# A depthwise convolution cut into steps and emitted between the weight products of its mixer

## The chip, the cores and the metric

The kernel runs on one core of a Trainium2 chip. The metric is the time of one execution on the device, in microseconds (us). The engines are written as the profile writes them: PE (matrix products; PEld its weight loads), DVE (vector engine), ACT (scalar engine), POOL (GpSimd), SP (here only the issuer of weight transfers). The engines run side by side; each works through its own instructions strictly in order and waits where it needs another engine's result.

## What is computed

The program is two two-layer transformer blocks over 256 rows of width 1024, in float32. The change touches one piece, the mixer of the second layer of the second block (the "odd mixer"):

```
def odd_mixer(u, conf_dw, conf_dw_b, conf_ln_g, conf_ln_b, sc_dw):
    a, gate, sb, scc, sx = jnp.split(u, [512, 1024, 1536, 2048], axis=-1)
    conf = a * jax.nn.sigmoid(gate)
    conf = depthwise_conv(conf, conf_dw) + conf_dw_b            # 31 taps
    conf = jax.nn.silu(group_layer_norm(conf, conf_ln_g, conf_ln_b, 4))
    sc = sb * depthwise_conv(scc * sx, sc_dw)                   # 3 taps
    return jnp.concatenate([conf, sc], axis=-1)
...
mix = odd_mixer(h @ b_w_in[j], ...) @ b_w_out[j]                # 1024x2560, 1024x1024
x = x + g1 * mix
```

## The kernel before

`phase_f` holds this layer. A float32 product is made of three products of rounded parts. So each weight tile of 1 MB (`w`, a ring of 4 slots, filled from SP's queue) is cut in two sub-steps, and each sub-step is **split**: ACT writes the rounded half `whi` (line 200), then POOL or DVE writes the rest `wlo` = `w` - `whi` (line 201, 128x1024). Three buffers of each are held (`NSPL`), so at most three sub-steps are split ahead of PE. In `lin_T` POOL does the `wlo` of every sub-step; in `residual` (through `products`) DVE does it. After each weight tile one step of a background job is pumped in: eight products `ada<-w,cs` with a 1 MB tile of their own; after eight steps comes `ada_sb` (DVE), then four transposes of it on PE, then `adaT` (DVE).

The input product `h @ b_w_in` goes as five calls of `lin_T`, each of two weight tiles, four sub-steps, 96 products of 256 columns: **c2=0** (gate and value of channel groups 0 and 1), **c2=1** (groups 2 and 3), **scc**, **sx**, **sb**. I number their sub-steps s1 to s4 (of c2=1), scc1 to scc4, sx1 to sx4, sb1 to sb4. A channel group is 128 channels on the partitions with the 256 rows beside each other, so a tap of the convolution is one DVE instruction over 128x256 (`SCALAR_TENSOR_TENSOR ocv<-oconf,cw,ocv`, line 1916): shifted input times the tap's weight plus the sum so far. Two of the 31 taps (`TAPS`) go over PE instead (`oconv<-odw,oconf`, line 1939), one is a DVE `TENSOR_SCALAR` with the bias (line 1918), 28 are left per group. They are emitted in the evictions: when the value of two groups is ready, DVE makes `oconf` = value * sigmoid(gate) (line 1934) and then all the taps of these two groups. The three-tap convolution `osv` is emitted in the eviction of sx in the same way.

After all five calls the sums `ocv` of the four groups are added onto PE's part in PSUM (line 1963, transposing them), `head_norm` normalizes 128 rows x 4 groups at a time (statistics, a reciprocal root of 10 small instructions on `hr_t`, `hr_y`, `hr_a`, then `oct`), PE transposes back (`oT`), ACT applies Silu (`osl`), and the result is split into `lhs_hi` and `lhs_lo` for `residual`. That one multiplies by `b_w_out`, four weight tiles in the order (half of the columns, first row block) = (0,4), (1,4), (0,0), (1,0); rows 4 to 7 come from `osv`, 0 to 3 from the normalized groups. I call its eight sub-steps r1 to r8 (12 products of 512 columns each).

A scheduler orders the emitted instructions engine by engine, so the order on an engine is near the order of emission but not the same.

Of the kernel before, what the change touches and what calls it, by code (L numbers as in the profile page):

```python
# [132 lines left out]
class Kernel:  # L133
# [23 lines left out]
    def rsqrt(self, v, eps, shape, scale=1.0, name="rs", bufs=4):  # L157

        nc = self.nc
        t = self.small(shape, name + "_t", bufs=bufs)  # L160
        y = self.small(shape, name + "_y", bufs=bufs)
        a = self.small(shape, name + "_a", bufs=bufs)
# [57 lines left out]
    def products(self, W, nk, steps, lhs, tts, evict):  # L220
# [4 lines left out]
        for c, cols, k0, kn in steps:  # L225
# [6 lines left out]
            for s0 in range(k0, k0 + kn, sub):  # L232
# [5 lines left out]
                for tt in tts:  # L238
# [1384 lines left out]
    def residual(self, W, nk, lhs, L, which):  # L1623

        nc = self.nc
        self.pump_to(self.ada[2 + L], 1 + which)
        with self.pool("res") as p:
            o = 2048 + 3072 * which
            g = self.bcast(p, self.ada[2 + L].dram[0, o:o + 1024], D, "gres")

            def ev(c, tt, ps):
                sl = slice(c * 512, c * 512 + 512)
                gy = self.sb.tile([128, 512], F32, name="gy", tag="s512")
                nc.vector.tensor_mul(gy, ps, g[:, sl])
                (nc.vector if c in RA else nc.gpsimd).tensor_add(self.xres[tt][:, sl], self.xres[tt][:, sl], gy)
            if nk == 8:
# [216 lines left out]
    def lin_T(self, W, cols, lhs, evict, eng):  # L1853
# [6 lines left out]
        for k0 in range(0, 8, per):  # L1860
            w = self.wtile(W, k0, per, cols)
            self.pump(self.rate)
            for s0 in range(0, per, sub):
                wh, wl = self.split(w[:, s0:s0 + sub], sub, n, eng)
                for k in range(sub):
                    kk = k0 + s0 + k
                    for c in range(n // 128):
# [2 lines left out]
                        nc.tensor.matmul(o, wh[:, k, cs], hi[:, kk], start=kk == 0 and c % 2 == 0, stop=False)  # L1870
                        nc.tensor.matmul(o, wh[:, k, cs], lo[:, kk], start=False, stop=False)  # L1871
                        nc.tensor.matmul(o, wl[:, k, cs], hi[:, kk], start=False, stop=kk == 7 and c % 2 == 1)  # L1872
        for i, a in enumerate(acc):
            evict(i, a)

    def phase_f(self):
# [3 lines left out]
        with ExitStack() as s:  # L1880
# [5 lines left out]
            with self.pool("pf") as p:  # L1886
# [13 lines left out]
                pv = [self.psB("oconv") for _ in range(2)]  # L1900
# [8 lines left out]
                scc = p.tile([128, 4, 256], F32, name="oscc")  # L1909

                def conv(dst, src, c, taps, w0, bias):
                    for k in taps:
                        w = cw[:, c, w0 + k:w0 + k + 1]
                        x = src[:, c, k:k + 256]
                        if k > taps[0]:
                            V.scalar_tensor_tensor(dst[:, c], x, w, dst[:, c], op0=OP.mult, op1=OP.add)  # L1916
                        elif bias is not None:
                            V.tensor_scalar(dst[:, c], x, w, bias, op0=OP.mult, op1=OP.add)
                        else:
                            V.tensor_scalar(dst[:, c], x, w, None, op0=OP.mult)  # L1920

                def each(ev):
                    def pair(i, ps):
# [4 lines left out]
                def ev_conf(c2):  # L1928
                    def ev(i, ps):
# [2 lines left out]
                            nc.scalar.activation(sg[:, c], ps, AF.Sigmoid)  # L1932
                            return
                        V.tensor_mul(conf[:, c, 15:271], ps, sg[:, c])
                        conv(cv, conf, c, range(TAPS, 31), 0, self.pcol[:, 53 + c:54 + c])
                        for t in range(2):
                            for k in range(TAPS):
                                at = k + t * 128
                                nc.tensor.matmul(pv[t][:, c * 128:c * 128 + 128], conf[:, c, at:at + 128],
                                                 dw[:, c, k], start=c == 0 and k == 0, stop=False)  # L1940
# [4 lines left out]

                def ev_sx(c, ps):
                    V.tensor_mul(scx[:, c, 1:257], ps, scc[:, c])
                    conv(sv, scx, c, range(3), 31, None)

                def ev_sb(c, ps):  # L1950
                    V.tensor_mul(sv[:, c], ps, sv[:, c])
                    self.split_T(mix[0][:, 4 + c], mix[1][:, 4 + c], sv[:, c])

                for c2 in range(2):
                    self.lin_T(W, ((512 + 256 * c2, 256), (256 * c2, 256)), lhs, each(ev_conf(c2)), nc.gpsimd)
                self.lin_T(W, ((1536, 512),), lhs, each(ev_scc), nc.gpsimd)
# [3 lines left out]
                ct = [p.tile([128, 512], F32, name=f"oct{t}") for t in range(2)]  # L1960
                for t in range(2):
                    for c in range(4):
                        nc.tensor.matmul(pv[t][:, c * 128:c * 128 + 128], cv[:, c, t * 128:t * 128 + 128],
                                         self.ident, start=False, stop=c == 3)
                    self.head_norm(pv[t], ct[t], True, 1e-6)
                for c in range(4):
                    po = self.psB("oT")
                    for t in range(2):
                        self.tr(po[:, t * 128:t * 128 + 128], ct[t][:, c * 128:c * 128 + 128])
                    u = self.sb.tile([128, 512], F32, name="osl", tag="s512")  # L1970
                    nc.scalar.activation(u[:, :256], po[:, :256], AF.Silu, scale=self.pcol[:, 57 + c:58 + c],
                                         bias=self.pcol[:, 61 + c:62 + c])
                    self.split_T(mix[0][:, c], mix[1][:, c], u[:, :256])
            self.residual(I["b_w_out_2"][0], 8, mix, 1, 0)
            for t in range(2):
                self.dump("x2_mid1", self.xres[t], t)
            self.ffn(1)
# [1 line left out]
    def build(self, s, upto="all"):  # L1979
# [62 lines left out]
```

## Time and profile before

| | |
|---|---|
| median of 3 runs | 2436.0 us (2433.91 to 2442.73) |
| the profiled execution: its time, and the span from first to last instruction | 2441.86 us, 2439.7 us |
| busy share of PE, DVE, ACT, POOL | 91%, 51%, 29%, 22% |
| mean granted clock of PE | 0.951 of full speed |

The shares are means over the whole program. What the changed stage is worth has to be read from its own stretch, from about 2111 us (the first two groups of the convolution can begin) to about 2241 us (the next layer part begins). All times below are us from the start of the span.

### The profile page before, as it was taken

Reading aid. Unit: us, or ns where it says so; the run is one execution under the profiler, and the core shown is the slowest. Engines: PE = TensorE matmul, PEld = TensorE weight load, DVE = VectorE, ACT = ScalarE, POOL = GpSimd, SP = SyncE. Lnnn points to the kernel's source line nnn. Section 1 sums busy time; section 2 is a strip of 40 time slices with the busy share of each in tenths; the row PEclk is TensorE's granted clock in tenths of the full one; section 3 lists DMA queues with packets and bytes.
Section 4 is the critical chain, followed back from the end, with each engine's and each line's share of the span. In section 5 each row is a group of like instructions: output and inputs, shape, how many; then the busy total and the mean of one; then the engine's idle time right before and its main releaser. Section 6 shows DMA issues by size and latency. Waiting matters only on the chain. (4 is left out here: it accounts for less than half of the span.)

```text
span 2439.7 us, 35230 instructions
## 1 busy us (share of the span) xinstructions
PE 2218.6 (91%) x13185; PEld 1395.5 (57%) x13186; DVE 1254.7 (51%) x2724; ACT 708.4 (29%) x1179; POOL 537.6 (22%) x451
## 2 busy tenths in 40 slices
PE   7999995789999998899779999998899999858999
PEld 3786673444444443676633333332655998657997
DVE  3354767444444444757842322223774554666554
ACT  2215242111111111434421111111453543414442
POOL 2121334233333333300130211111201000561000
PEclk9999996699999999899979999999899999979999
DMA  8654365389999999443569999999554555737553
GB/s 301 249 193 156 134 213 223 129 342 408 408 409 409 409 408 373 155 173 132 191 240 384 409 408 408 409 409 380 190 191 172 191 176 186 261 107 274 186 179 120
DMA packets 209272, 652.36 MB, mean 267 GB/s; under 512 B 20668, under 2 KB 33965, under 8 KB 197568
## 3 DMA queue, kind: packets, MB, share of 16 engines
q1 hardware_dynamic: 201680, 632.24, 68.9%
q0 software_dynamic: 7408, 17.73, 2.2%
q8 instruction: 107, 1.75, 0.3%
q14 instruction: 77, 0.63, 0.1%
HBM read 648.65 MB, written 1.25 MB: 266 GB/s over the span
## 5 line engine op out<-in xcount | busy, mean ns | idle before, releaser
L825 PE MATMUL gu<-w,xT 128*32 128x512 f32 (+1 forms) x2880 | 493.0, 605 | 16.2 <-PEq L967 9.9
L201 DVE TENSOR_TENSOR wlo<-w,whi 128x1024 fp32r<-128x1024 f32 (+3 forms) x240 | 298.7, 1246 | 308.6 <-ACT whi L200 308.4
L200 ACT ACTIVATE whi<-w 128x1024 fp32r<-128x1024 f32 (+3 forms) x264 | 274.2, 1041 | 508.4 <-PE A L247 276.8
L825 PEld LDWEIGHTS gu<-w,xT 128*32 128x32 f32 (+1 forms) x2880 | 141.0, 121 | 315.5 <-issue 246.4
L1872 PE MATMUL A<-lhs_hi,wlo 128*128 128x256 f32 x864 | 246.5, 286 | 14.1 <-POOL wlo L201 13.6
L246 PE MATMUL A<-wlo,lhs_hi 128*128 128x512 f32 (+3 forms) x640 | 248.7, 389 | 9.5 <-DVE wlo L201 9.4
L245 PE MATMUL A<-whi,lhs_hi 128*128 128x512 f32 (+3 forms) x640 | 250.6, 396 | 5.9 <-ACT whi L200 2.8
L1870 PE MATMUL A<-lhs_hi,whi 128*128 128x256 f32 x864 | 247.8, 287 | 1.0 <-ACT whi L200 1.0
L1871 PE MATMUL A<-lhs_lo,whi 128*128 128x256 f32 x864 | 247.1, 286 | 0.0
L247 PE MATMUL A<-whi,lhs_lo 128*128 128x512 f32 (+3 forms) x640 | 246.6, 386 | 0.0
L876 POOL TENSOR_TENSOR mx<-mx,gy 128x512 f32<-128x512 f32 x124 | 161.5, 1331 | 355.0 <-DVE gy L875 354.9
L851 PE MATMUL ey<-w,hT 128*32 128x512 f32 (+1 forms) x1440 | 225.8, 595 | 9.5 <-ACT hT L838 9.5
L875 DVE TENSOR_TENSOR gy<-sc,g 128x512 f32<-128x512 f32 x188 | 121.5, 685 | 218.2 <-PE sc L872 215.8
L1872 PEld LDWEIGHTS A<-lhs_hi,wlo 128*128 128x128 f32 x864 | 167.8, 194 | 14.5 <-POOL wlo L201 13.8
L1870 PEld LDWEIGHTS A<-lhs_hi,whi 128*128 128x128 f32 x864 | 167.9, 195 | 7.1 <-issue 5.0
L1871 PEld LDWEIGHTS A<-lhs_lo,whi 128*128 128x128 f32 x864 | 168.0, 194 | 0.2 <-DVE lhs_lo L255 0.2
L876 POOL TENSOR_TENSOR xres<-xres,gy 128x512 f32<-128x512 f32 x58 | 74.3, 1293 | 380.0 <-DVE gy L875 379.1
L245 PEld LDWEIGHTS A<-whi,lhs_hi 128*128 128x128 f32 x640 | 123.1, 194 | 56.3 <-issue 17.7
L851 PEld LDWEIGHTS ey<-w,hT 128*32 128x32 f32 (+1 forms) x1440 | 68.3, 120 | 147.9 <-issue 115.6
L246 PEld LDWEIGHTS A<-wlo,lhs_hi 128*128 128x128 f32 x640 | 123.4, 193 | 39.6 <-DVE wlo L201 13.8
L748 PE MATMUL xT<-Pm,uh 128*128 128x256 f32 (+1 forms) x416 | 111.4, 303 | 29.4 <-DVE Pm L736 29.4
L247 PEld LDWEIGHTS A<-whi,lhs_lo 128*128 128x128 f32 x640 | 123.5, 193 | 24.2 <-issue 4.0
(586 smaller groups left out, 3264.8 us busy)
## 6 DMA issues: line engine op xcount, KB each, us to landing
w<-in_moe_w_gate_dram SPq DMA_DIRECT2D x248, 512.0 KB, 10.2
w<-in_moe_w_up_dram SPq DMA_DIRECT2D x248, 512.0 KB, 10.2
w<-in_moe_w_down_dram SPq DMA_DIRECT2D x248, 512.0 KB, 10.2
w<-in_ada_w_dram SPq DMA_DIRECT2D x88, 1024.0 KB, 6.7
w<-in_ffn_w_dram SPq DMA_DIRECT2D x64, 1024.0 KB, 5.1
w<-in_ab_w_in_dram SPq DMA_DIRECT2D x13, 1024.0 KB, 9.0
w<-in_c_w_qkv_dram SPq DMA_DIRECT2D x12, 1024.0 KB, 5.2
w<-in_ada_w_dram SPq DMA_DIRECT2D x16, 512.0 KB, 9.9
```

What stands on the lines that cost most here:

```text
L200: self.nc.scalar.activation(hv, w, AF.Copy)
L201: (eng or self.nc.vector).tensor_sub(lv, w, hv.bitcast(F32))
L245: nc.tensor.matmul(o, hi[:, kk, ts], wh[:, k], start=at + k == 0, stop=False)
L246: nc.tensor.matmul(o, hi[:, kk, ts], wl[:, k], start=False, stop=False)
L247: nc.tensor.matmul(o, lo[:, kk, ts], wh[:, k], start=False, stop=at + k == nk - 1)
L825: nc.tensor.matmul(pgu[m][a:b], xT[:, j, a:b], w[:, i, k], start=j == 0, stop=j == 7)
L851: nc.tensor.matmul(py[h][a:b], hT[:, j, a:b], w[:, i, k, h * 512:h * 512 + 512], start=j == 0, stop=j == 3)
L875: V.tensor_mul(gy, ps, M.g2[t // 2][:, h * 512:h * 512 + 512])
L876: eng.tensor_add(o, o, gy)
L1870: nc.tensor.matmul(o, wh[:, k, cs], hi[:, kk], start=kk == 0 and c % 2 == 0, stop=False)
L1871: nc.tensor.matmul(o, wh[:, k, cs], lo[:, kk], start=False, stop=False)
L1872: nc.tensor.matmul(o, wl[:, k, cs], hi[:, kk], start=False, stop=kk == 7 and c % 2 == 1)
```

## The change

The convolution of a channel group becomes a generator, `conv_norm(c)`, that yields after every tap and between the parts of its own layer norm. The evictions of c2=0 and c2=1 only put the generators in a queue, `between`. After each sub-step of `lin_T` and `products`, `aside` advances the queue by `SHARE` = 7 steps, changing between the two groups at its head. The layer norm is done group by group, 2 row blocks x 1 group. The bias tap, and the first tap of the three-tap convolution, go from DVE to ACT. In `residual`, the row blocks 0 to 3 come in four tiles of half the size, (0,0,2), (1,0,2), (0,2,2), (1,2,2), and `self.early = 8` gives the `wlo` of all eight sub-steps to POOL instead of DVE.

```diff
+SHARE = 7
+CONV_STEPS = (0, 4, 4), (1, 4, 4), (0, 0, 2), (1, 0, 2), (0, 2, 2), (1, 2, 2)
...
+    def aside(self):
+        b = self.between
+        for _ in range(self.share):
+            while b and next(b[0], 0) == 0:
+                b.popleft()
+            if len(b) > 1:
+                b[0], b[1] = b[1], b[0]
...
                         if k > taps[0]:
                             V.scalar_tensor_tensor(dst[:, c], x, w, dst[:, c], op0=OP.mult, op1=OP.add)
+                            yield
                         elif bias is not None:
-                            V.tensor_scalar(dst[:, c], x, w, bias, op0=OP.mult, op1=OP.add)
+                            nc.scalar.activation(dst[:, c], x, AF.Identity, scale=w, bias=bias)
                         else:
-                            V.tensor_scalar(dst[:, c], x, w, None, op0=OP.mult)
+                            nc.scalar.activation(dst[:, c], x, AF.Copy, scale=w)
+
+                def conv_norm(c):
+                    yield from conv(cv, conf, c, range(TAPS, 31), 0, self.pcol[:, 53 + c:54 + c])
+                    pv = self.psB("oconv")
+                    for t in range(2):
+                        o = pv[:, t * 128:t * 128 + 128]
+                        for k in range(TAPS):
+                            at = k + t * 128
+                            nc.tensor.matmul(o, conf[:, c, at:at + 128], dw[:, c, k], start=k == 0, stop=False)
+                        nc.tensor.matmul(o, cv[:, c, t * 128:t * 128 + 128], self.ident, start=False, stop=True)
+                    st = self.small([128, 4, 6], "hn_st")
+                    mv = self.small([128, 4, 2], "hn_mv")
+                    for t in range(2):
+                        V.bn_stats(st[:, t], pv[:, t * 128:t * 128 + 128])
+                        V.bn_aggr(mv[:, t], st[:, t])
+                    yield
+                    yield
+                    r = self.rsqrt(mv[:, :2, 1], 1e-6, [128, 2], name="hr")
+                    ct = self.sb.tile([128, 512], F32, name="oct", tag="s512")
...
+                    for t in range(2):
+                        V.tensor_scalar(ct[:, t * 128:t * 128 + 128], pv[:, t * 128:t * 128 + 128],
+                                        mv[:, t, 0:1], r[:, t:t + 1], op0=OP.subtract, op1=OP.mult)
+                    po = self.psB("oT")
...
+                    self.split_T(mix[0][:, c], mix[1][:, c], u[:, :256])
+                    yield
...
                         V.tensor_mul(conf[:, c, 15:271], ps, sg[:, c])
-                        conv(cv, conf, c, range(TAPS, 31), 0, self.pcol[:, 53 + c:54 + c])
...
+                        self.between.append(conv_norm(c))
...
                     V.tensor_mul(scx[:, c, 1:257], ps, scc[:, c])
-                    conv(sv, scx, c, range(3), 31, None)
+                    sc.append(conv(sv, scx, c, range(3), 31, None))
...
+                self.between.extendleft(reversed(sc))
                 self.lin_T(W, ((1024, 512),), lhs, each(ev_sb), nc.gpsimd)
...
-            self.residual(I["b_w_out_2"][0], 8, mix, 1, 0)
+                self.early = 8
+                self.residual(I["b_w_out_2"][0], 8, mix, 1, 0, CONV_STEPS)
+                assert not self.between
```

Three places show what this makes of the engines' orders (line numbers of the changed kernel differ from those of before).

First, DVE from the first two groups of `oconf` on. Before:

```order
L1934 TENSOR_TENSOR oconf<-A,osg 128x256 x2
L1918 TENSOR_SCALAR ocv<-oconf,cw,pcol 128x256 x2
L1916 SCALAR_TENSOR_TENSOR ocv<-oconf,cw,ocv 128x256 x56
L1934 TENSOR_TENSOR oconf<-A,osg 128x256 x2
L1918 TENSOR_SCALAR ocv<-oconf,cw,pcol 128x256 x2
L1916 SCALAR_TENSOR_TENSOR ocv<-oconf,cw,ocv 128x256 x56
L317 TENSOR_TENSOR ada_sb<-ada,ada_sb 128x512
L1947 TENSOR_TENSOR oscx<-A,oscc 128x256 x2
L325 COPY adaT_1114<-ada 128x16 x2
```

Now:

```order
L1983 TENSOR_TENSOR oconf<-A,osg 128x256 x2
L1930 SCALAR_TENSOR_TENSOR ocv<-oconf,cw,ocv 128x256 x27
L1983 TENSOR_TENSOR oconf<-A,osg 128x256
L1930 SCALAR_TENSOR_TENSOR ocv<-oconf,cw,ocv 128x256
L1983 TENSOR_TENSOR oconf<-A,osg 128x256
L1930 SCALAR_TENSOR_TENSOR ocv<-oconf,cw,ocv 128x256 x34
L328 TENSOR_TENSOR ada_sb<-ada,ada_sb 128x512
L1930 SCALAR_TENSOR_TENSOR ocv<-oconf,cw,ocv 128x256 x2
L336 COPY adaT_1114<-ada 128x16 x2
L1930 SCALAR_TENSOR_TENSOR ocv<-oconf,cw,ocv 128x256 x8
L1950 BN_STATS hn_st<-oconv 128x6 x2
```

The taps still stand in long runs. `oconf` of groups 2 and 3 moved from behind 56 taps to behind 27 and 28, and `ada_sb` from behind 112 taps to behind 62. On PE the four transposes of `ada_sb` stood behind the whole of sx; now they stand inside its first sub-step, after nine of its 24 products:

```order
L1883 MATMUL A<-lhs_hi,whi 128x256
L1884 MATMUL A<-lhs_lo,whi 128x256
L1885 MATMUL A<-lhs_hi,wlo 128x256
L154 MATMUL ada<-ident,ada_sb 128x128 x4
L1883 MATMUL A<-lhs_hi,whi 128x256
L1884 MATMUL A<-lhs_lo,whi 128x256
L1885 MATMUL A<-lhs_hi,wlo 128x256
```

Before, PE's place that needed the convolution's input was inside scc, the two taps of groups 2 and 3:

```order
L1871 MATMUL A<-lhs_lo,whi 128x256
L1872 MATMUL A<-lhs_hi,wlo 128x256
L1939 MATMUL oconv<-odw,oconf 128x128 x8
L1870 MATMUL A<-lhs_hi,whi 128x256
L1871 MATMUL A<-lhs_lo,whi 128x256
L1872 MATMUL A<-lhs_hi,wlo 128x256
```

Second, ACT in c2=1 and scc. Before, only sigmoids, splits and copies stand there:

```order
L1932 ACT_TABLE_LOAD
L1932 ACTIVATE osg<-A 128x256 x2
L200 ACTIVATE whi<-w 128x1024 x4
L1932 ACTIVATE osg<-A 128x256 x2
L200 ACTIVATE whi<-w 128x1024 x4
L1944 ACTIVATE oscc<-A 128x256 x2
```

Now the bias taps stand between the splits:

```order
L1981 ACTIVATE osg<-A 128x256 x2
L201 ACTIVATE whi<-w 128x1024
L1933 ACTIVATE ocv<-oconf,pcol,cw 128x256 x2
L201 ACTIVATE whi<-w 128x1024 x3
L1981 ACTIVATE osg<-A 128x256 x2
L201 ACTIVATE whi<-w 128x1024
L1933 ACTIVATE ocv<-oconf,pcol,cw 128x256 x2
L201 ACTIVATE whi<-w 128x1024 x3
```

The second pair of them needs `oconf` of groups 2 and 3, and the splits of scc4, sx1 and sx2 are queued behind it.

Third, DVE from the eviction of sx to the start of `residual`. Before:

```order
L1920 TENSOR_SCALAR osv<-oscx,cw 128x256 x2
L1916 SCALAR_TENSOR_TENSOR osv<-oscx,cw,osv 128x256 x4
L1947 TENSOR_TENSOR oscx<-A,oscc 128x256 x2
L1920 TENSOR_SCALAR osv<-oscx,cw 128x256 x2
L1916 SCALAR_TENSOR_TENSOR osv<-oscx,cw,osv 128x256 x4
L201 TENSOR_TENSOR wlo<-w,whi 128x1024 x2
L1951 TENSOR_TENSOR osv<-A,osv 128x256 x3
L255 TENSOR_TENSOR lhs_lo<-osv,lhs_hi 128x256 x3
```

Now:

```order
L1991 TENSOR_TENSOR oscx<-A,oscc 128x256
L266 TENSOR_TENSOR lhs_lo<-osl,lhs_hi 128x256 x2
L1991 TENSOR_TENSOR oscx<-A,oscc 128x256 x3
L1930 SCALAR_TENSOR_TENSOR osv<-oscx,cw,osv 128x256 x8
L1930 SCALAR_TENSOR_TENSOR ocv<-oconf,cw,ocv 128x256 x21
L1995 TENSOR_TENSOR osv<-A,osv 128x256 x4
L1930 SCALAR_TENSOR_TENSOR ocv<-oconf,cw,ocv 128x256
L266 TENSOR_TENSOR lhs_lo<-osv,lhs_hi 128x256 x4
L1930 SCALAR_TENSOR_TENSOR ocv<-oconf,cw,ocv 128x256 x2
```

The eviction of sb (`osv<-A,osv`) and the `lhs_lo` that r1 needs now stand behind 8 taps of `osv` and 21 of `ocv`; before, behind 8 of `osv` and two `wlo`.

## Rows read from the trace of the kernel before

**Rows 1.** The page: span, and the chain that ended last, by line.

```profile
span 2439.7 us, 35230 instructions
...
DMA w<-in_moe_w_up_dram 11%; DMA w<-in_moe_w_down_dram 5%; PE A L1872 4%; PE A L1870 4%; PE A L1871 4%; PE A L246 3%; PE A L247 3%; PE A L245 3%; DVE ocv L1916 2%; POOL wlo L201 1%; PE ada L313 1%; PE mo L1838 1%; PE ms L1823 1%; DVE wlo L201 1%; PE aT L152 1%; PE gu L825 1%
```

**Rows 2.** Waits in 2080 to 2250: in total, times, longest.

```profile
PE A L1872 <- POOL wlo L201: 13.6, 1, 13.6
...
PE oconv L1939 <- DVE oconf L1934: 13.1, 1, 13.1
```

**Rows 3.** Timeline, DVE: start, us, instruction, count, idle before.

```profile
2111.43 0.76 DVE L1934 TENSOR_TENSOR oconf<-A,osg 128x256 f32<-128x256 f32 x2 [7.37 <-PE A L1872]
...
2112.75 37.23 DVE L1916 SCALAR_TENSOR_TENSOR ocv<-oconf,cw,ocv 128x256 f32<-128x256 f32 x56
...
2151.21 22.26 DVE L1916 SCALAR_TENSOR_TENSOR ocv<-oconf,cw,ocv 128x256 f32<-128x256 f32 x56
...
2186.34 0.76 DVE L1947 TENSOR_TENSOR oscx<-A,oscc 128x256 f32<-128x256 f32 x2 [12.27 <-PE A L1872]
```

**Rows 4.** Line 1916 and line 201, 2112.7 to 2138: ns min/median/max.

```profile
L1916 DVE SCALAR_TENSOR_TENSOR ocv<-oconf,cw,ocv x25: 470/475/2620, 2112.7 to 2135.1; 128x256 f32<-128x256 f32 x25
...
L201 POOL TENSOR_TENSOR wlo<-w,whi x7: 2392/2603/2719, 2113.6 to 2135.0; 128x1024 fp32r<-128x1024 f32 x7
```

**Rows 5.** Timeline, POOL.

```profile
2107.57 4.77 POOL L201 TENSOR_TENSOR wlo<-w,whi 128x1024 fp32r<-128x1024 f32 x2 [0.32 <-ACT whi L200]
2113.62 2.64 POOL L201 TENSOR_TENSOR wlo<-w,whi 128x1024 fp32r<-128x1024 f32 x1 [1.27 <-ACT whi L200]
...
2156.10 24.23 POOL L201 TENSOR_TENSOR wlo<-w,whi 128x1024 fp32r<-128x1024 f32 x3 [18.68 <-ACT whi L200]
```

**Rows 6.** Stretches: PE, PEld, DVE, ACT, POOL busy (instructions), clock, DMA share, GB/s.

```profile
2120.97:2126.90 5.93, 5.93 (x52) 5.81 (x48) 5.93 (x8) 1.76 (x4) 4.24 (x2) 1.00 0.83 309
2126.90:2127.90 1.00, 1.00 (x9) 0.16 (x8) 1.00 (x1) 1.00 (x2) 0.93 (x1) 1.00 0.63 262
...
2221.23:2226.90 5.67, 5.67 (x28) 4.43 (x24) 3.64 (x6) 3.19 (x6) 0.00 (x0) 1.00 0.85 331
2204.50:2233.60 29.10, 27.91 (x136) 19.07 (x133) 20.26 (x61) 13.14 (x18) 2.54 (x2) 1.00 0.89 316
2233.60:2240.60 7.00, 1.69 (x13) 0.56 (x13) 6.98 (x30) 3.51 (x9) 1.17 (x2) 0.93 0.92 319
```

**Rows 7.** Stretches after PE's waits of 13.1 and 13.6 us, and one behind it.

```profile
2150.40:2153.80 3.40, 3.40 (x17) 3.40 (x17) 3.40 (x10) 0.00 (x0) 0.00 (x0) 0.50 0.00 0
2175.70:2181.40 5.70, 5.67 (x26) 5.68 (x27) 0.00 (x0) 0.39 (x1) 4.63 (x2) 0.50 0.85 292
2181.40:2192.50 11.10, 11.10 (x94) 11.10 (x93) 0.76 (x2) 3.87 (x4) 8.77 (x4) 0.99 0.64 230
```

**Rows 8.** Groups by line and shape, 2111 to 2236: count, busy us, mean ns.

```profile
L201 DVE TENSOR_TENSOR wlo<-w,whi 128x1024 fp32r<-128x1024 f32 x10 | 12.7, 1276 | 6.5 <-ACT whi L200 6.5
...
L1918 DVE TENSOR_SCALAR ocv<-oconf,cw,pcol 128x256 f32<-128x256 f32 x4 | 1.4, 402 | 0.0
...
L200 ACT ACTIVATE whi<-w 128x1024 fp32r<-128x1024 f32 x25 | 26.4, 1062 | 85.1 <-PE A L1871 41.3 <-DMA w<-in_b_w_in_dram 19.1 <-DMA w<-in_b_w_out_dram 12.5
...
L1932 ACT ACTIVATE osg<-A 128x256 f32<-128x256 f32 x4 | 1.3, 381 | 1.2 <-PE A L1872 1.2
```

**Rows 9.** Timeline, DVE and POOL: a small step that was stopped, small steps alone.

```profile
2084.87 5.09 DVE L178 SCALAR_TENSOR_TENSOR rs_y<-rs_a,rs_y 128x1 f32<-128x1 f32 x1
...
2085.29 4.64 POOL L201 TENSOR_TENSOR wlo<-w,whi 128x1024 fp32r<-128x1024 f32 x2
...
2214.74 0.16 DVE L175 TENSOR_TENSOR hr_a<-hr_a,hr_t 128x4 f32<-128x4 f32 x1
2214.94 0.16 DVE L180 SCALAR_TENSOR_TENSOR hr_a<-hr_a 128x4 f32<-128x4 f32 x1
```

**Rows 10.** DMA issues of 2180 to 2240: count, KB each, us to landing.

```profile
w<-in_b_w_out_dram SPq DMA_DIRECT2D x4, 1024.0 KB, 8.3
```

More of the change, by code (lines that the diff above doesn't have):

```diff
@@ L159, in rsqrt @@
         nc = self.nc
-        t = self.small(shape, name + "_t", bufs=bufs)
-        y = self.small(shape, name + "_y", bufs=bufs)
-        a = self.small(shape, name + "_a", bufs=bufs)
+        room = [128, 4] if name == "hr" else shape
+        t, y, a = (self.small(room, name + k, bufs=bufs)[:, :shape[1]] for k in ("_t", "_y", "_a"))
         k = 0.703952253
@@ L250, in products @@
                 done[c] = at + sn
+                self.aside()
+    def aside(self):
[5 more added lines that the diff above has]
+                b[0], b[1] = b[1], b[0]
     def split_T(self, hi, lo, u, eng=None):
@@ L1621, in rms_affine, with residual @@
             self.affine_T(xr, lambda i, j: A[:, i, j:j + 1], lambda i, j: ada.T[:, i, o + j:o + j + 1], lhs)
-    def residual(self, W, nk, lhs, L, which):
+    def residual(self, W, nk, lhs, L, which, steps=None):
         nc = self.nc
@@ L1635, in ev @@
                 (nc.vector if c in RA else nc.gpsimd).tensor_add(self.xres[tt][:, sl], self.xres[tt][:, sl], gy)
-            if nk == 8:
+            if steps:
+                self.products(W, 8, [(c, ((c * 512, 512),), k, n) for c, k, n in steps], lhs, (0, 1), ev)
+            elif nk == 8:
                 self.lin_D(W, lhs, (0, 1), ev, (4, 0), BOTH[1 + L])
@@ L1872, in lin_T @@
                         nc.tensor.matmul(o, wl[:, k, cs], hi[:, kk], start=False, stop=kk == 7 and c % 2 == 1)
+                self.aside()
         for i, a in enumerate(acc):
@@ L1899, in phase_f @@
                         nc.scalar.activation(dw[:, c, k], self.ident, AF.Copy, scale=cw[:, c, k:k + 1])
-                pv = [self.psB("oconv") for _ in range(2)]
                 conf = p.tile([128, 4, 286], F32, name="oconf")
@@ new lines, in conv_norm @@
+                def conv_norm(c):
[17 more added lines that the diff above has]
+                    yield
+                    yield
+                    yield
+                    for t in range(2):
+                        V.tensor_scalar(ct[:, t * 128:t * 128 + 128], pv[:, t * 128:t * 128 + 128],
+                                        mv[:, t, 0:1], r[:, t:t + 1], op0=OP.subtract, op1=OP.mult)
+                    po = self.psB("oT")
+                    for t in range(2):
+                        self.tr(po[:, t * 128:t * 128 + 128], ct[:, t * 128:t * 128 + 128])
+                    u = self.sb.tile([128, 512], F32, name="osl", tag="s512")
+                    nc.scalar.activation(u[:, :256], po[:, :256], AF.Silu, scale=self.pcol[:, 57 + c:58 + c],
+                                         bias=self.pcol[:, 61 + c:62 + c])
+                    self.split_T(mix[0][:, c], mix[1][:, c], u[:, :256])
+                    yield
@@ L1934, in ev @@
                         V.tensor_mul(conf[:, c, 15:271], ps, sg[:, c])
-                        conv(cv, conf, c, range(TAPS, 31), 0, self.pcol[:, 53 + c:54 + c])
[L1936 to L1940, printed above, removed]
+                        self.between.append(conv_norm(c))
                     return ev
@@ L1952, in ev_sb @@
                     self.split_T(mix[0][:, 4 + c], mix[1][:, 4 + c], sv[:, c])
+                sc = []
                 for c2 in range(2):
@@ L1957, in phase_f @@
                 self.lin_T(W, ((2048, 512),), lhs, each(ev_sx), nc.gpsimd)
+                self.between.extendleft(reversed(sc))
                 self.lin_T(W, ((1024, 512),), lhs, each(ev_sb), nc.gpsimd)
[L1960 to L1973, printed above, removed]
-            self.residual(I["b_w_out_2"][0], 8, mix, 1, 0)
+                self.early = 8
+                self.residual(I["b_w_out_2"][0], 8, mix, 1, 0, CONV_STEPS)
+                assert not self.between
             for t in range(2):
@@ L1991, in build @@
         self.early = 0
+        self.between, self.share = deque(), SHARE
         self.cap = CAPS[0]
```

## The prediction

> **What bounds the kernel now.** I read the page first. The chain of waits ends in PE's products and in weight transfers of other layers; the convolution is about 2% of 2439.7 us [rows 1]. So only the stage is worth reading, from 2111.4 (first `oconf` [rows 3]) to 2240.6, where the next layer part begins [rows 6]: 129 us.
>
> Then the waits of that stage. PE stands still twice: 13.1 us until DVE gives `oconf` of groups 2 and 3, and 13.6 us until POOL gives the `wlo` of sx2 [rows 2]. Each has an after-effect: PE comes back at a granted clock of 0.50 (1.2 of 2.4 GHz), for 3.4 us and more after the first and 5.7 us after the second; there 26 records took 5.7 us where 94 take 11.1 us later [rows 7]. That is 0.22 against 0.12 us each, some 2.6 us lost per restart.
>
> Then I asked what DVE and POOL do to each other, because a tap reads two arrays from SBUF, and so does a `wlo`. The same 56 taps took 37.23 us in the first run and 22.26 us in the second [rows 3]; seven `wlo` ran inside the first [rows 4], and hardly one got in during the second. So a tap costs 22.26/56 = 0.40 us alone, and each `wlo` costs the run (37.23 - 22.26)/7 = 2.14 us. The tap under a `wlo` takes up to 2.62 us instead of 0.47 [rows 4]. A `wlo` undisturbed takes 2.39 us (4.77 for two [rows 5]). It also goes the other way: of the three `wlo` from 2156.10 to 2180.33 the first had to wait for the end of the second run, 24.23 us for three instead of 7.2 [rows 5]; that is PE's second wait. **The two engines take turns.** What reads one array from SBUF is outside this: `oconf` beside the `wlo` of 2107.57 to 2112.34 took 0.76 for two [rows 3, 5].
>
> On this the Trainium skill (SBUF — State Buffer, Who interferes with whom) says that a VectorE instruction with two SBUF inputs contends with a GpSimd instruction that reads SBUF, and that the second to issue blocks until the first has finished. The trace agrees in kind; not in the long wait, which outlasted more than forty taps. By the page a `wlo` would cost DVE its whole 2.39 us, and the forecast below would be 22 x 0.25 = 5.5 us later.
>
> **The shared time, before the steps.** From the first tap to the end of `residual` the change keeps 112 + 8 taps (120 x 0.40 = 48 us) and has 22 `wlo` on POOL (s3, s4, then 4 for each of scc, sx, sb, and 8 in `residual`): 22 x 2.14 = 47 us. Before, there were 14 on POOL (30 us) and 8 in `residual` on DVE at 1.28 [rows 8] (10 us). So the pair must take turns for 95 us instead of 88, while PE's own work in this stretch is 4 calls x (2 x 5.93 + 2 x 1.0) + 4 x 5.67 + 4 = 82 us [rows 6] and some 8 us of transposes and taps, 90 in all. Adding what else DVE must do there (evictions, statistics, normalization, some 17 us at 0.15 to 0.4 us each) the pair needs about 112 us. **Spreading the taps cannot make PE the bound here; it decides only where PE waits.** I follow the five places.
>
> **Step by step.** (1) *c2=1, scc.* The bias taps leave DVE (4 x 0.40 [rows 8]) and go to ACT. The trace has no such ACT row; the nearest is 0.38 (`osg` [rows 8]), the upper bound the 1.06 of a `whi`; I take 0.4, hidden, but what stands behind them is not. The first taps wait for ACT, and the `wlo` of 2113.62 gets in ahead of them: first tap at about 2116.1 instead of 2112.8. PE, without 16 product records of `oconv` (1.7 us), ends c2=1 at 2125.3 instead of 2126.9. Four `wlo` (s4, scc1 to scc3) fall in the next 14 us, so n taps: 14 = 0.40 n + 4 x 2.14, n = 14, at 2130. Now ACT holds the bias taps of groups 2 and 3, which need `oconf`, behind taps 27 and 28: 14 more at 0.40 and two `oconf` at 0.38, until 2136.4. Behind them on ACT wait the `whi` of scc4, sx1, sx2. Then 0.8 + 1.06 (ACT) + 2.39 (`wlo`): scc4 at 2141, where PE wanted it at 2136.3. **Wait 4.7.**
>
> (2) *`ada_sb`.* PE does scc4, a step of ada and nine products of sx1, to about 2146, and then needs `ada_sb`, behind tap 62. From 2136.4 that is 34 x 0.40 = 13.6, four `wlo` (scc4, sx1 to sx3) = 8.6, and 0.7 (two reads at 0.38 as the measure): 2159.3. **Wait 13.** Cost: this replaces the 13.1 of before. The 13.6 behind `wlo` goes, since sx1 to sx3 are split by now.
>
> (3) *Layer norm of groups 0 and 1.* PE restarts at half clock, ends sx1 and the `oconv` products at 2165, sx2 and sx3 at 2171.3; inside sx4 it needs `oct` of group 0. DVE gets its statistics from PE at 2164.4, is held by sx4's `wlo` until 2166.5, then statistics (1 us) and eleven taps with some twenty small steps between them. Small steps alone are 0.20 us apart [rows 9], under a tap about 0.1: 11 x 0.40 + 20 x 0.15 = 7.4. Two `wlo` (sb1, sb2) get in: 4.3. `oct` at 2179. **Wait 7.5.** A small step with two inputs can be stopped too: one stood 5.09 us behind two `wlo` [rows 9].
>
> (4) *sb into `residual`.* PE ends sx at 2185 (before: the eviction of its first half began at 2186.34 [rows 3]), sb at 2199, and with ada is at r1 at 2200.3. DVE must do 8 + 21 taps from 2187.4 (11.6) with five `wlo` (sb4, r1 to r3 and most of sb3: 10.7), the eviction of sb (4 x 0.38) and a `lhs_lo`: 2211. **Wait 10.7.** Before, r1 began at 2204.5 [rows 6].
>
> (5) *`residual`.* Before, 29.1 us from r1 to the last product [rows 6], and 7.0 more to the next part. Now: 4 x 5.67, four steps of ada (4.0; one of them lay in the 7.0 before), transposes and `oconv` 2.9, one restart at half clock 2.6, and the group norms of 2 and 3, just in time: 32.5. Last product at 2211 + 32.5 = 2243.5 against 2233.6. The 7.0 behind it become about 6.3. The half tiles change no product count. **The next part begins some 9 us later, at 2250.**
>
> The FFN behind it is the same instructions. 2441.9 + 9 = 2451 for an execution like the profiled one, which was 5.9 above the median of the three. Step 4 has a cheaper form (below), so I take +8 on the median: **2444 us**, of its own 2437 to 2452. Half a per cent of 2436 is 12 us, about what a measurement of this kernel can tell from no change.
>
> **Rivals.** *Taps fit into gaps (faster).* PE's waits were 26.7 us, its restarts 5; if all of it went and nothing came, the stage is PE-bound and ends 28 us earlier: 2408 to 2424 with one small wait left. For that the pair must stay under PE's 90 us: beside 65 us of DVE a `wlo` may cost DVE no more than (90 - 65)/22 = 1.1 us. Against it: seven of seven cost 2.14. For it: the gaps of DVE after 2173 (12.27 before sx's eviction [rows 3]) are now used, and my arrival times carry errors of some us each. Chance 0.16.
>
> *DVE keeps POOL out.* In the second run it did, once for 19 us [rows 5]. If it does so in the run of 29, `wlo` of sb4 comes at 2203, sb ends 2206.5 and r1 starts at 2207.5, not 2211; steps 1 and 2 end alike, because PE then waits for `wlo` while the taps run. 2436 + 4 = 2440. Chance 0.20.
>
> *Late half tiles and stopped small steps (slower).* A 1 MB tile landed 8.3 us after its issue [rows 10]. In `residual` six tiles of weights and six of ada go through four slots, two weight tiles ahead; with half tiles a step lasts 2.84 + 1.0, so two steps are 7.7 us. If r6, r7 and r8 each wait 2 to 4 us, or each of the four norms is stopped by one more `wlo` (2.4), the end is 6 to 12 us later still: 2450 to 2460. For it: DMA was already 0.83 to 0.89 busy there [rows 6]. Against: half of each tile's bytes are gone. Chance 0.19.
>
> **Numbers.** The forecast has 0.45. Faster by over 0.5%: the first rival, 0.16. Within: two thirds of the forecast (0.31), the second rival (0.20), a little of the third: 0.54. Slower: the rest, 0.30. For 8 in 10 the range leaves out most of the first rival and the end of the third: 2420 to 2458.
>
> **What would show it.** Right: taps of 2.6 us wherever a `wlo` runs, in all four calls; a wait of PE for `ada_sb` near 2146 of about 13 us (step 2), one for `oct` in sx (step 3), one at the first products of `residual` behind `osv` or `lhs_lo` (step 4); r1 later than 2204.5; PE at 0.50 after each. Wrong: `wlo` and taps side by side at their own lengths; PE busy through sx and sb and sb ended before 2190; or `residual` starting as early as before, with the norm of groups 2 and 3 hidden. Then the stage ends before 2240 and the first rival holds.

## The result, and the profile after

The changed kernel takes 2447.02 us (median of 12 runs, 2444.67 to 2455.1), the kernel before 2435.64 (12 runs). The ratio is 1.0053, 95% interval 1.0041 to 1.0065: a loss of 11 us, small and real. The profiled execution has a span of 2452.3 us against 2439.7 [rows 1]. From the first `oconf` to the next layer part it needs 145.3 us (2109.11 to 2254.45) instead of 129.2 [rows 3, 6]; ahead of this stage it was 2.3 us faster, behind it 1.2. So the stage holds the whole difference. What stands ahead of it and behind it is the same work in both kernels; I read the 3.5 us there as scatter between two executions; the stage alone grew by 16 us.

The waits of PE, 2080 to 2260: engine, line, waited for, us in total, times, longest.

```profile
PE aT L154 <- DVE xr L1630: 16.3, 2, 10.3
PE A L1885 <- POOL wlo L202: 13.6, 1, 13.6
PE oT L154 <- DVE oct L1960: 11.0, 2, 9.6
PE A L246 <- ACT lhs_hi L265: 9.1, 1, 9.1
PE A L1883 <- ACT whi L201: 1.5, 1, 1.5
PE ada L154 <- DVE ada_sb L328: 0.8, 1, 0.8
```

In place of the two waits of before [rows 2] there are three long ones: the first for POOL's `wlo` of scc4, the second for `oct` (9.6 us), the third at r1, the first step of `residual`. To these comes a tail of 10.3 us behind the last product (the longest of the first row). DVE's timeline shows what stands behind the first two:

```profile
2109.11 0.76 DVE L1983 TENSOR_TENSOR oconf<-A,osg 128x256 f32<-128x256 f32 x2 [7.38 <-PE A L1885]
2111.47 21.23 DVE L1930 SCALAR_TENSOR_TENSOR ocv<-oconf,cw,ocv 128x256 f32<-128x256 f32 x27 [1.61 <-ACT ocv L1933]
...
2133.69 13.53 DVE L1930 SCALAR_TENSOR_TENSOR ocv<-oconf,cw,ocv 128x256 f32<-128x256 f32 x34
2155.03 0.69 DVE L328 TENSOR_TENSOR ada_sb<-ada,ada_sb 128x512 f32<-128x512 f32 x1 [7.81 <-POOL wlo L202]
...
2167.05 6.06 DVE L1930 SCALAR_TENSOR_TENSOR ocv<-oconf,cw,ocv 128x256 f32<-128x256 f32 x1
```

Twenty-seven taps with five `wlo` beside them: 27 x 0.40 + 5 x 2.1 = 21.3, the law of the prediction. Then 34 taps at 0.40 each, with no `wlo` among them, though one was due: its `whi` was ready at 2135.4, after POOL had waited 7.36 us for it. POOL's timeline has it, and the end of the stage:

```profile
2135.43 18.66 POOL L202 TENSOR_TENSOR wlo<-w,whi 128x1024 fp32r<-128x1024 f32 x3 [7.36 <-ACT whi L201]
...
2168.18 4.64 POOL L202 TENSOR_TENSOR wlo<-w,whi 128x1024 fp32r<-128x1024 f32 x2
...
2239.17 1.16 POOL L330 DMA_DIRECT2D adaD<-ada_sb  x2 [3.65 <-DVE ada_sb L328]
2240.91 1.28 POOL L1646 TENSOR_TENSOR xres<-xres,gy 128x512 f32<-128x512 f32 x1 [0.58 <-DVE rA L1624]
2248.11 0.59 POOL L270 DMA_DIRECT2D gres<-adaD  x1 [5.91 <-issue]
2248.72 1.28 POOL L1646 TENSOR_TENSOR xres<-xres,gy 128x512 f32<-128x512 f32 x1
```

Three `wlo` in 18.66 us where three alone take 7.2: the first, scc4's, took 14.0 us, until DVE's run was over. PE stood still behind it. The tap of 6.06 us is the reverse: it was held by two `wlo` back to back (4.64 us). At the end the second `xres` add stands in POOL's queue behind the DMA of the next `gres`, ahead of which POOL stood 5.91 us.

The stretches by stage (first `oconf` to `ada_sb`, to `oscx`, to r1, `residual`, tail); the first column is PE's busy time, PEclk the granted clock:

```profile
2109.11:2155.00 45.89, 30.80 (x233) 25.68 (x226) 36.47 (x66) 11.70 (x17) 32.49 (x9) 0.85 0.52 194
2155.00:2183.16 28.16, 18.57 (x133) 15.95 (x134) 25.02 (x61) 7.81 (x11) 12.75 (x10) 0.82 0.52 188
2183.16:2208.30 25.14, 16.12 (x130) 13.01 (x128) 25.14 (x38) 7.34 (x11) 12.34 (x5) 0.92 0.62 230
2208.30:2244.20 35.90, 34.39 (x156) 23.58 (x156) 21.91 (x53) 10.14 (x14) 14.40 (x8) 0.91 0.63 216
2244.20:2254.45 10.25, 0.00 (x1) 0.01 (x1) 6.20 (x23) 3.62 (x9) 1.88 (x2) 0.71 0.48 168
sum 145.34, PE 99.89 PEld 78.24 DVE 114.74 ACT 40.61 POOL 73.84; mean PE 19.98 PEld 15.65 DVE 22.95 ACT 8.12 POOL 14.77
```

DVE is busy for 114.7 of 145.3 us, and all the time from `oscx` to r1, while PE works 16 of 25 us there: ahead of `residual` the pair DVE and POOL sets the pace, not PE. In `residual` PE works 34.4 of 35.9 us.

### The profile page after: what moved, and what is told of

It is laid out like the page before. It is cut to its first block, busy times and chain, and to the rows that moved or that the text cites. A ratio compares the mean times of both kernels' runs of the same rounds, so it can differ in the third digit from the quotient of the medians.

```text
span 2452.3 us, 35254 instructions
## 1 busy us (share of the span) xinstructions
PE 2222.4 (91%) x13185; PEld 1395.4 (57%) x13186; DVE 1269.2 (52%) x2728; ACT 712.2 (29%) x1187; POOL 550.0 (22%) x459
## 5 line engine op out<-in xcount | busy, mean ns | idle before, releaser
L202 DVE TENSOR_TENSOR wlo<-w,whi 128x1024 fp32r<-128x1024 f32 (+3 forms) x232 | 289.1, 1247 | 298.5 <-ACT whi L201 298.3
L1885 PE MATMUL A<-lhs_hi,wlo 128*128 128x256 f32 x864 | 246.9, 286 | 14.1 <-POOL wlo L202 13.6
```

Of the source, the lines that this page charges most:

```text
L202: (eng or self.nc.vector).tensor_sub(lv, w, hv.bitcast(F32))
```

## Experiments

Three questions. Is it the turns of DVE and POOL that set the stage, or the order of the queues? What did the interleaving itself bring? Which parts of the change lost the 11 us? All times are medians; the stage is that from first `oconf` to the next layer part in each profile, since its start differs by up to 12 us (2099.7 in e3, 2111.4 before) between profiles of kernels that are alike ahead of it. A profile is one execution, and not always one near the median: that of e4b was the longest of its six, 2432.4 us.

| kernel | what | us | ratio to before, 95% | stage, us | PE busy in it |
|---|---|---|---|---|---|
| before | | 2435.6 | | 129.2 | 96.0 |
| after | the change | 2447.0 | 1.0041 to 1.0065 | 145.3 | 99.9 |
| e1 | `residual` splits on DVE | 2441.1 | 1.0014 to 1.0034 | 139.3 | 100.8 |
| e2 | `xres` adds on DVE | 2448.1 | 1.0032 to 1.0070 | 141.8 | 100.3 |
| e5 | first taps on DVE | 2443.3 | 1.0021 to 1.0046 | 141.2 | 99.4 |
| e13 | e1, e2, e5 together | 2434.1 | 0.9981 to 1.0003 | 129.9 | 99.0 |
| e3 | after, tap sums in PSUM | 2418.0 | 0.9917 to 0.9949 | 116.1 | 94.5 |
| e9 | before, tap sums in PSUM | 2409.3 | 0.9875 to 0.9913 | 105.6 | 93.6 |
| e4 | after, all splits on DVE | 2414.4 | 0.9904 to 0.9937 | 112.5 | 94.8 |
| e8 | e4 and e2 | 2409.6 | 0.9876 to 0.9915 | 109.1 | 95.0 |
| e4b | before, all splits on DVE | 2424.9 | 0.9938 to 0.9967 | 124.0 | 94.9 |

**Is it the turns? e3: the sums of the taps in PSUM.**

```
 def conv_norm(c):
-    yield from conv(cv, conf, c, range(TAPS, 31), 0, bias)
     pv = self.psB("oconv")
+    yield from conv(cv, conf, c, range(TAPS, 31), 0, bias, pv[:, 256:])
...
-V.scalar_tensor_tensor(dst[:, c], x, w, dst[:, c], ...)
+o = dst[:, c] if acc is None or k == taps[-1] else acc
+V.scalar_tensor_tensor(o, x, w, dst[:, c] if acc is None else acc, ...)
```

> The running sum of the 29 taps of a group stands in PSUM (the free half of the group's `oconv` bank), so that a tap reads one operand from SBUF and one from PSUM; the last tap writes `cv` in SBUF as before. Order, engines and counts are unchanged. Theory A (taps and `wlo` take turns because both read two operands from SBUF): taps beside a `wlo` go on at about 0.4 us, POOL's first `wlo` of scc4 no longer waits 14 us, PE's waits of 13.6 and 9.6 us fall below 5 together, time 2422 to 2432. Theory B (order of the queues alone): the waits stay, time 2445 to 2450. Theory C (a tap with its sum in PSUM is dearer, 0.5 us or more, and sets the stage itself): waits move to the groups' ends, time 2440 to 2455.

2417.95 us, below the range of theory A and far from B and C. The groups of the tap's line and of POOL's `wlo`, 2100 to 2216 (ns minimum/median/maximum):

```profile
L1931 DVE SCALAR_TENSOR_TENSOR oconv<-oconf,cw,oconv x108: 473/481/490, 2102.3 to 2182.0; 128x256 f32<-128x256 f32 x108
L1931 DVE SCALAR_TENSOR_TENSOR osv<-oscx,cw,osv x8: 472/474/2625, 2155.5 to 2162.3; 128x256 f32<-128x256 f32 x8
...
L202 POOL TENSOR_TENSOR wlo<-w,whi x23: 2361/2399/2523, 2098.2 to 2196.2; 128x1024 fp32r<-128x1024 f32 x23
```

In the changed kernel the same taps took up to 6.06 us and a `wlo` up to 14.0. With the sum in PSUM no tap out of 108 took over 0.49 us and no `wlo` over 2.52. The eight taps of `osv`, which still read both arrays from SBUF, took up to 2.63. Same order, same engines, same counts: the turns of these taps cost 29 us of the 2447. The Trainium skill (SBUF — State Buffer, Who interferes with whom) says that a VectorE instruction with at most one SBUF input, outside its modes with two ports, does not contend with GpSimd; these rows agree.

e3 is not wholly without turns: the eight taps of `osv` stood in one run of 9.39 us, where eight at 0.40 take 3.2, and PE then waited 6.1 us for `lhs_hi` at r1.

```profile
2155.52 9.39 DVE L1931 SCALAR_TENSOR_TENSOR osv<-oscx,cw,osv 128x256 f32<-128x256 f32 x8 [2.80 <-ACT osv L1936]
```

**The same from the other side, e4: all 28 splits on DVE.**

```
-self.lin_T(W, ..., lhs, each(ev_...), nc.gpsimd)
+self.lin_T(W, ..., lhs, each(ev_...), V)
...
-self.early = 8
+self.early = 0
```

> All 28 weight splits of this stage (20 of the lin_T products, 8 of the residual) on DVE instead of POOL. Theory A: a `wlo` costs DVE 1.22 to 1.28 us on its own engine in place of 2.14 us of shared time, 24 us less in all; PE's waits inside the stage fall by 10 to 20 us, time 2424 to 2436. Theory B (sharing costs nothing; DVE's own queue is the bound): 28 x 1.25 = 35 us more work on DVE, time 2465 to 2485.

2414.35 us, below theory A's range again. DVE's timeline:

```profile
2109.57 2.85 DVE L1930 SCALAR_TENSOR_TENSOR ocv<-oconf,cw,ocv 128x256 f32<-128x256 f32 x7
2113.51 0.76 DVE L1983 TENSOR_TENSOR oconf<-A,osg 128x256 f32<-128x256 f32 x2 [1.09 <-PE A L1885]
2114.18 1.22 DVE L202 TENSOR_TENSOR wlo<-w,whi 128x1024 fp32r<-128x1024 f32 x1
2115.31 2.86 DVE L1930 SCALAR_TENSOR_TENSOR ocv<-oconf,cw,ocv 128x256 f32<-128x256 f32 x7
2118.09 1.22 DVE L202 TENSOR_TENSOR wlo<-w,whi 128x1024 fp32r<-128x1024 f32 x1
```

Seven taps (`SHARE`), one `wlo`, seven taps: here the interleaving does what it says. Giving DVE 28 more splits made the kernel 33 us faster. A `wlo` on DVE costs it 1.22 us, and one on POOL among taps cost it 2.14: by these prices 28 x 0.92 = 26 us, an estimate of DVE's time, not of the kernel's. The rest is not split up here; the 14.0 us for which POOL was kept out are gone as well.

**What is the interleaving worth without turns? e9: before, with sums in PSUM; e4b: before, with the splits on DVE.** The edits are those of e3 and e4 in the old order, but that e9's sums have PSUM banks of their own, where e3's stand in the free half of the group's `oconv` bank.

> The kernel before, taps in whole runs, with each group's running sum of taps in a PSUM bank and only the last tap writing `cv` in SBUF; splits stay on POOL. Theory A: taps take 0.40 to 0.48 us also beside a `wlo`, both runs of 56 end within some 26 us, POOL is not held, PE's waits of 13.6 and 13.1 us ahead of the layer norm go, and the time is 2412 to 2422: most of what the changed kernel gained by the same edit (2418 us) comes without any interleaving. Theory B (the interleaving is what hides the taps): the waits stay within 5 us of what they were, 2430 to 2440.

> The kernel before, with the 20 weight splits of this stage's lin_T products on DVE instead of POOL (its residual's eight are there already); taps in whole runs of 56, as before. Nothing on POOL takes turns with the taps now, but each `wlo` stands in DVE's own queue. Theory A1 (order counts once nothing is shared: a `wlo` behind 56 taps of 0.40 us comes some 15 us after PE wants it, twice): time 2430 to 2448, so that interleaving is worth 15 to 30 us against the same splits between taps put among the steps (2414 us). Theory A2 (order hardly counts even then; only shared time did): 2410 to 2422.

e9 takes 2409.3 us: theory A, and better than it said. The changed kernel with its sums in PSUM (e3) is 8.7 us slower. PE's waits in e9, 2080 to 2260:

```profile
PE aT L152 <- DVE xr L1619: 9.7, 2, 6.0
PE ada L313 <- DMA w<-in_ada_w_dram: 3.5, 2, 2.9
PE A L245 <- ACT whi L200: 2.4, 1, 2.4
```

The waits of 13.1 and 13.6 us [rows 2] are gone without any interleaving in the program. e4b takes 2424.9, between the two ranges: 10.5 us slower than the interleaved e4, less than theory A1 said. Its waits, and its first run of taps:

```profile
PE oconv L1963 <- DVE ocv L1916: 13.0, 1, 13.0
PE ada L313 <- DMA w<-in_ada_w_dram: 8.2, 2, 6.3
PE A L1872 <- DVE wlo L201: 4.5, 1, 4.5
...
2108.79 22.25 DVE L1916 SCALAR_TENSOR_TENSOR ocv<-oconf,cw,ocv 128x256 f32<-128x256 f32 x56
```

The last row settles the price: the first run of 56 taps, which took 37.23 us beside seven `wlo` of POOL [rows 3, 4], takes 22.25 with none. The 8.2 us for a transfer stand in e4b's longest execution; whether its other runs have them is not known.

Where a `wlo` stands in DVE's own queue, the order decides when it comes, and the interleaved kernel is 10 us faster. With sums in PSUM the old kernel was the faster one. Neither pair differs in the order alone: in both the interleaved kernel has its first taps on ACT and half tiles in `residual`, and in the second pair its eight last splits on POOL besides.

**Which parts lost? e1, e2, e5, one edit each.** e1 and e5 undo a part of the change. e2 does not: the `xres` adds of the first half were on POOL in the kernel before as well, where they stood in a row ahead of the DMA transfers:

```profile
2227.30 2.54 POOL L1635 TENSOR_TENSOR xres<-xres,gy 128x512 f32<-128x512 f32 x2 [25.68 <-DVE gy L1634]
```

The new order of `residual` brings them later. The edits, in this order:

```
-self.early = 8
+self.early = 0
...
-(nc.vector if c in RA else nc.gpsimd).tensor_add(self.xres[tt][:, sl], ...)
+(nc.vector if c in RA or steps else nc.gpsimd).tensor_add(self.xres[tt][:, sl], ...)
...
-nc.scalar.activation(dst[:, c], x, AF.Identity, scale=w, bias=bias)
+V.tensor_scalar(dst[:, c], x, w, bias, op0=OP.mult, op1=OP.add)
...
-nc.scalar.activation(dst[:, c], x, AF.Copy, scale=w)
+V.tensor_scalar(dst[:, c], x, w, None, op0=OP.mult)
```

> One part of the change undone: the eight weight splits of the residual's product go back to DVE, as in the kernel before; taps and layer norms stay between the steps. Theory A (DVE's two-input operations and POOL's `wlo` take turns; each `wlo` on POOL costs DVE 2.14 us of shared time, one on DVE 1.22): the small steps are no longer stopped, first residual step to last product falls from 35.9 us to 29-32, time 2440 to 2444. Theory B (the order of the queues alone makes the loss, sharing costs nothing): DVE gets 8 x 1.22 us more work on the path, time 2448 to 2455.

> Both residual adds of the first column half go from POOL to DVE, in this residual alone. If the second add was late because it stood behind the next `gres` DMA in POOL's queue (5.9 us with no releaser shown), the tail from last product to the next `aT` falls from 10.3 us to about 6.3, time 2442 to 2444. If instead the end of the tail is set by something else (the `rA` products or the clock at half), the tail stays at 9 to 10 us and the time at 2446 to 2448.

> The changed kernel with the eight first taps (bias taps of the two convolutions) back on DVE in place of ACT. If ACT's first taps hold `whi` back and so make the wait at scc4 (first step of the forecast), it shortens by up to 4.7 us, time 2441 to 2444. If POOL's `wlo` is kept out by DVE's run of taps there, as the trace of the changed kernel reads, the wait of 13.6 us stays or grows by the added DVE work (about 0.5 us), time 2446 to 2450.

e1: 2441.1, theory A; its interval lies below that of the changed kernel, so the splits on POOL cost some 6 us. They cost them in another place than I had said: `residual` went from 35.9 to 34.1 us only, and PE's wait at r1 from 9.1 to 2.6. The reading, which no run tests by itself: the `wlo` of the first steps no longer take turns with the last taps ahead of r1.

e2: the tail fell from 10.3 to 6.2 us, so the queue behind `gres` was its cause; the time did not show it (2448.1, with an interval that holds a gain of 5 us as well as a loss of 4). r1 stood 1.9 us later in its stage (101.1 us behind the first `oconf`, 99.2 in the changed kernel). What the adds cost by themselves stays open.

e5: 2443.3, in the first range, but its interval touches that of the changed kernel. And it is not the way I had written: the wait at scc4 did not shorten, it went (nine `wlo` got in among the first 28 taps, scc4's with them), and another took its place. So ACT's first taps do hold `whi` back, and by that the `wlo` came late enough to be kept out:

```profile
PE ada L154 <- DVE ada_sb L328: 13.5, 1, 13.5
...
PE A L246 <- ACT lhs_hi L265: 8.6, 1, 8.6
PE oT L154 <- DVE oct L1960: 5.9, 2, 5.6
```

That is the wait of step 2 of the prediction, 13 us, though in a kernel that has no bias taps on ACT, so the agreement in size is no test of its sum.

**e13: the three edits together.** What is left of the change is the order of taps and layer norms and the half tiles of `residual`. One edit is more than an undoing: the adds of the first half are on DVE, where the kernel before has them on POOL.

> The changed kernel with its three moves between engines undone together (first taps on DVE, the residual's splits on DVE, the adds of its first half on DVE): what is left of the change is the order of the taps and of the layer norms. If the interleaving as such neither gains nor loses while taps and `wlo` take turns, and the loss of 11 us was these moves (6 for the splits, 4 for the first taps, up to 4 for the adds), the time is that of the kernel before, 2431 to 2439. If the moves hid a gain of the interleaving, 2420 to 2430. If the interleaving itself loses, 2440 to 2446.

2434.1 us, ratio 0.9992 (0.9981 to 1.0003): the time of before. So the new order, with the adds taken out of POOL's queue, neither gains nor loses, and the 11 us are gone with the two moves between engines and the place of the adds. How much of it the adds are is open: e1 and e5 account for some 6 and 4 us by their medians, e2 for none, and e1 and e5 together without e2 were not run. PE's waits in e13:

```profile
PE ada L154 <- DVE ada_sb L328: 13.5, 1, 13.5
PE aT L154 <- DVE xr L1630: 6.6, 1, 6.6
PE aT L154 <- DVE rs_y L182: 6.1, 1, 6.1
PE oT L154 <- DVE oct L1960: 5.6, 1, 5.6
PE A L1883 <- DVE oconf L1983: 3.1, 1, 3.1
PE A L246 <- ACT lhs_hi L265: 2.1, 1, 2.1
```

**Looking for a faster one. e8: e4 and e2 together.**

> The changed kernel with all 28 splits on DVE and in addition the residual adds of the first column half on DVE, so that POOL's queue with the `gres` DMA is off the end of the stage. If the two edits are worth what each showed alone, the tail of 11.5 us falls to about 6, time 2407 to 2411. If the tail's end is set elsewhere, 2413 to 2416.

2409.6 us as expected; the tail is 7.1 us. PE is at work for 38 of the 40 us ahead of `residual`, so little is left to hide there. **e10, e11, e12: e3 with other edits** (e10: the edits of e1 and e2 on top; e11: the one below; e12: all of these).

```
-SHARE = 7
+SHARE = 16
```

> The changed kernel with the sums of the taps in PSUM (2418 us by itself), and the residual's splits and its first half's adds on DVE, so that POOL has nothing in the residual. If what the interleaved order still loses against the order of before with the same sums (2409 us) lies in the residual and its tail, where 8 `wlo` and the `gres` DMA stand on POOL: 2409 to 2414. If it lies ahead of the residual (the two `osv` taps of each group, still with both operands in SBUF, took 9.4 us for 8 there, and `lhs_hi` came 6.1 us late): 2414 to 2418.

> The changed kernel with the sums in PSUM, and `SHARE` 16 in place of 7: taps and layer norms are drained more than twice as fast, so that less of them is left beside the last products and the residual. If spreading them thin is what the interleaved order loses (its work ends later than it could), r1 starts earlier and the time is 2409 to 2414. If the order of the queue makes no difference once taps are not held, 2416 to 2420.

> Both edits of the two kernels beside it: sums in PSUM, `SHARE` 16, the residual's splits and adds on DVE. If both causes hold and add up: 2403 to 2409, below the order of before with sums in PSUM (2409). If only one of them holds, as that one's run.

All three missed. e10 takes 2419.8 (0.9917 to 0.9945), no gain over e3, though its tail fell to 6.7 us. e11 takes 2425.8 and e12 2424.7 (0.9940 to 0.9971 and 0.9936 to 0.9968): draining faster looks worse, by 5 to 8 us in the medians, with intervals that overlap those of e10 and e3 at their ends. e11's waits:

```profile
PE oconv L1946 <- DVE ocv L1931: 5.8, 1, 5.8
PE A L247 <- POOL wlo L202: 5.6, 2, 3.9
PE A L246 <- ACT lhs_hi L265: 3.2, 1, 3.2
```

The first of these is new: a group's `oconv` products are then in PE's queue ahead of its last taps on DVE, and weight products stand behind them. Why e3 loses 9 us to e9 is not settled. By their profiles r1 begins 73.9 us behind the first `oconf` in e3 and 65.6 in e9, and e3's tail of 10.7 us is 3.5 longer. The turns that are left in e3, at the taps of `osv`, are not far from that size (9.39 us in place of 3.2); with their sums in PSUM too it was not run. e10 took the tail away and won nothing: its `residual` took 37.2 us, e3's 31.5.

## Why the prediction was right, and where it was off

**The cause.** "Spreading the taps cannot make PE the bound here" held: e13 stands at the time of before, with the taps spread and the turns kept, and e3, e4 and e9 show that the turns are what keeps the stage from PE's time. The 112 us forecast for the pair compare with 108.5 us of DVE's time up to the last product, the time in which it was held included; that the two are near is in part luck, since the forecast charged every `wlo` 2.14 us, and those that ran while DVE stood still cost it nothing. The first rival named the right condition, that a `wlo` must cost DVE less: where e3 and e4 remove the turns, the times are 2418 and 2414, inside its 2408 to 2424. Its limit of 1.1 us is not confirmed: e4 gets there at 1.22.

**Steps 1 and 2.** Forecast 4.7 us for scc4's `wlo` and 13 for `ada_sb`; measured 1.5 for a `whi`, 13.6 for scc4's `wlo` and 0.8 for `ada_sb`: 15.9 against 17.7. The waiting was of the size forecast, through another door. The first half of step 1 held: ACT's `whi` of scc4 stood behind the bias taps, and POOL came to it 26.3 us behind the first `oconf` (forecast 2138.3 - 2111.4 = 26.9). Then step 1 let POOL in between the taps, and DVE's 34 taps kept it out. That was the second rival's mechanism, in the run of 34 and not in the run of 29 that it named, where five `wlo` got in at 2.40 to 2.53 us each; and it said that steps 1 and 2 would end alike, because PE then waits for `wlo`. With the first taps on DVE (e5, e13) a wait of 13.5 us for `ada_sb` appears instead. The reading is that PE cannot pass before that run of taps is over, at whichever of the two it waits.

**Steps 3 and 4.** Forecast 7.5 and 10.7 us, measured 9.6 and 9.1. r1 was put 99.6 us behind the first `oconf` (2211 - 2111.4); it came at 99.2. The waits on the way were off by some 2 us each, in both directions (-1.8, +2.1, -1.6); that r1 is off by 0.4 only is luck.

**Step 5** was too small twice. `residual` was put at 32.5 us and took 35.9. Two causes can be read: r1 took 8.6 us for 28 records of PE at a mean granted clock of 0.64, 2.9 over a step at full clock [rows 6], where 2.6 were allowed; and the norms of groups 2 and 3, called just in time, made PE wait 1.46 us for `oct`. The other 1.6 us stand in PE's own rows: the step of ada that this wait cut in two took 2.0 us where one takes 1.0, and the transposes and `oconv` products 3.5 where 2.9 were allowed. The tail was put at 6.3 us and took 10.3, because the forecast left out what stands in POOL's queue between the two adds: `gres` of the FFN. e2 shows that this is the 4 us. Together the stage was forecast 9 us longer and was 16.

**The number.** The cheaper step 4, for which the forecast took off 1 us, did not happen; the median rose by 11.4 where +8 was said. In the two profiles the stage was 7 us too short in the forecast, and 3.5 us of scatter outside it hid half of that; so the number was nearer than the steps. The interval (1.0041 to 1.0065) also tells 3 us from nothing, where the prediction allowed itself 12.

**The third rival.** Late half tiles did not show: PE's waits in `residual` are for `lhs_hi` and `oct`, none for a transfer. Its other half, small steps of the norms that a `wlo` stops, did show, twice, ahead of the 1.46 us:

```profile
2222.55 2.16 DVE L166 TENSOR_SCALAR hr_t<-hn_mv 128x2 f32<-128x2 f32 x1
...
2226.32 2.25 DVE L182 SCALAR_TENSOR_TENSOR hr_y<-hr_a,hr_y 128x2 f32<-128x2 f32 x1
```

Each ended with a `wlo` of POOL that ran beside it (2222.29 to 2224.68, 2226.18 to 2228.56); alone such a step takes 0.13 to 0.17. In e1, with these `wlo` on DVE, PE's wait for `oct` in `residual` is gone. The first of the two steps reads one array only. So the prediction's sentence that what reads one array from SBUF is outside the turns holds for `oconf`, from whose rows it was read, and not for this step.

## What to carry to other kernels

When two engines take turns, put their times in one sum before thinking of order: where the sum exceeded what the third engine needs, as here, interleaving only chose where that engine waits. Look then for an operand that takes one of them out of the turns (here a running sum in PSUM, 26 us off the kernel before with a few edited lines), or move the work onto the one engine that must wait anyway if it is cheaper there (1.22 against 2.14 us). Once the turns are gone, the order has to be tried anew: the interleaved kernel was 10 us faster with all splits on DVE and 9 slower with the sums in PSUM, in pairs that differ by a little more than the order. And a move between engines that comes along with a new order is an edit of its own: here two of them (e1, e5) held most of the loss by their medians.

## What the runs showed of the hardware that I had not expected

A tap with its sum in PSUM lasts what a tap lasts alone, 0.47 to 0.49 us in 108 of 108 cases with 23 `wlo` in the same stretch. Where the taps of two groups alternate, they also follow each other as fast as from SBUF, 0.39 to 0.40 us. In e9 the first group's taps stand alone, each on the sum of the one before, and follow each other at 0.52 us:

```profile
2104.18 12.56 DVE L1917 SCALAR_TENSOR_TENSOR osum<-oconf,cw,osum 128x256 f32<-128x256 f32 x24
...
2141.08 17.32 DVE L1917 SCALAR_TENSOR_TENSOR osum<-oconf,cw,osum 128x256 f32<-128x256 f32 x44
```

Both runs have `wlo` of POOL beside them, so it is not the turns. No run here was read for one group alone with its sum in SBUF, so whether PSUM makes this dearer stays open.

Which engine gets in is not a matter of the next instruction: in the changed kernel a `wlo` was kept out by a run of 34 back-to-back taps and took 14.0 us, while in the run of 27 just before it five got in, at most 2.7 us each; in e13 nine got in among the first 28 taps and none took over 2.65 us (in its second run of 28 POOL had none to start). What decides it I did not find; a plan should allow for both.
